# The output product of a mixer layer in three parts, the first as filling of the neighbourhood attention, and mixture-of-experts pairs opened before the previous pair is closed

## The chip, the cores and the metric

The kernel runs on one NeuronCore of a Trainium2 chip, in float32 inputs and outputs, as one launch. The metric is the device time of that launch in microseconds (us). Matrix products run on TensorE (PE in the profile, with its weight loads shown apart as PEld), elementwise work on VectorE (DVE), ScalarE (ACT) and GpSimd (POOL); SyncE (SP) issues nearly all of the DMAs. Each engine runs its own instructions in a fixed order and waits on semaphores.

## The reference, cut to what matters

The model is two blocks of two layers each, on 512 tokens of width 1024.

The first block's layers end in a mixture of experts where each expert chooses its tokens: 16 experts, 64 tokens each, inner width 512.

```
affinity = softmax(h @ w_router)
gate, idx = top_k(affinity.T, 64)                       # per expert
x_in = h[idx]                                           # 64 x 1024 per expert
y = (silu(x_in @ w_gate) * (x_in @ w_up)) @ w_down * gate
x = x + scatter_add(y, idx)
```

The second block's layers run four mixers on slices of 256 columns, side by side, and join them by one output product. There are 256 further tokens of context (`cx`), which are carried through layer 0 and serve only as keys and values in layer 1.

```
y_a = fourier_mix(...)                 # inputs 0..255 of the output product  (chunks 0, 1)
y_b = neighbourhood_attention(...)     # 256..511, 4 heads of 64             (chunks 2, 3)
y_c = spatial_gating(...)              # 512..767                            (chunks 4, 5)
y_d = diff_post(diff_latent(...))      # 768..1023, 4 heads of 64            (chunks 6, 7)
x  = x + g1 * (concat(y_a, y_b, y_c, y_d) @ w_out)
x  = x + g2 * (relu(h2 @ w_ff1)**2 @ w_ff2)
```

Before that, `ada_params` makes the modulation (g1 among them) from `silu(c) @ ada_w`, a product with a weight of 1024 x 6144 per layer.

## The kernel before, in words

**Number format.** Most weights and activations are split into a high and a low part (`wsplit`, `split`: a rounded copy on ACT, line 334 or 362, and the remainder on DVE, line 335 or 363), and a product is three matmuls (`mm3`: high by high, high by low, low by high, lines 353, 354, 356). The experts' weights are used unsplit, as plain float32; such a matmul shows as two PE instructions in the trace.

**Order of the work.** The kernel is written in a tile language. Python code traces instructions in an order; a scheduler then plays a timing model, gives each engine a fixed order (earlier traced work first among what its model holds ready) and puts each tile into one of the slots of its tag, as they come free. `k.fill(work, n)` steps a generator, so that pieces of other work are traced behind a given PE instruction. What the hardware does later can't change the order.

**Experts** (`experts`, from line 872; twice, once per layer). Four groups `g` of four experts. A group first gathers its tokens by a product with a one-hot matrix (line 888, 72 matmuls) and makes the gates and the transposed one-hot matrices (lines 899 to 915). Then it takes two pairs of experts. For each expert of a pair: gate and up product (line 930, both with 64 output columns, 32 PE instructions), a scaled copy to SBUF on ACT (`au`, 933), four transposes (936), silu on ACT (938) and a product on DVE (`gg`, 939). Then, for the pair, the down product (948): `G[h]` of the two experts write the two halves of the partitions of one PSUM tile, 32 PE instructions; its result is split (`yy`, 365 and 366), multiplied by the transposed one-hot matrix (956, 16 matmuls) and added to `x` (957). The weights come by DMA of 1 MiB (`we`, issued at line 288), 12 for a pair: 4 for each expert's gate and up and 4 for the pair's down weights. They have `NWE` = 14 slots in layer 0 and 12 in layer 1, at the right end of SBUF. Their rows in DRAM are 2 KB long.

**Second block** (`groups`, `na`, `diff`). After the projections, the neighbourhood attention `na` runs 24 units in layer 0 and 16 in layer 1 (a unit is one head and 128 queries): scores (1209, 1210; 256 columns each), bias add, softmax, four transposes (458), product with the values (492). Units alternate between the two heads of a pair `j`; the operands of the second pair are prepared at the first unit (`NAP`). Each pair's output goes through `parts` to chunks 2 and 3 of `YX` (and `YC` for the context).
Then `diff` runs as many units: two score tiles in PSUM (1292), two maxima (1295), two exponentials (1296), their combination (1302), six transposes and twelve value matmuls. Its first unit starts by `prepare`, which copies halves of queries and keys by DMA into stacked tiles (1252, tag `w`, 13 slots in all), and then `begin()`, which splits chunks 4, 5, 0, 1 with `parts`. From the third unit on it steps the output product: `adds` has 48 pieces, 8 output chunks `c` by 6 input chunks `e` (0 to 5), and `FILL[0]` = 2 are traced per unit. The rest follows behind `diff`, and then the last two input chunks (6, 7).
A piece is the three matmuls of `mm3` on 512 columns, and in layer 0 three more on the 256 context columns.

**PSUM** has 8 banks. `na` uses 4 for scores, 2 for transposes, 2 for outputs; `diff` 3 tiles of 2 banks (tag `pD`, which the pieces share) and 2.

Of the kernel before, what the change touches and what calls it, by code (L numbers as in the profile page):

```python
# [139 lines left out]
def layout(a):  # L140
# [18 lines left out]
    for n in ("ln_ffn", "sgu_ln_g_2", "sgu_ln_b_2", "sgu_b_2", "diff_lq1_2", "diff_lk1_2", "diff_lq2_2",  # L159
              "diff_lk2_2", "w_gate", "w_up", "w_down", "ada_w_2"):  # L160
        o[n] = a[n]
    for l in range(2):
# [23 lines left out]
        o[f"w2_out{l}"] = chunks(a["w_out_2"][l][:768], 2)  # L186
        o[f"w2_last{l}"] = chunks(a["w_out_2"][l][768:], 8)
# [12 lines left out]
NWE = (14, 12)  # L200
FIN = 0
NAP = 0
FILL = (2, 0, 0)
# [4 lines left out]
NAB = 7  # L208
# [10 lines left out]
HEADS = {"h": 18, **NORMS}  # L219
MIX = {"f": 4, "e": 3, "pt": 4, "sqm": 3, "lat": 6, "kg": 4, "qk": 12, "kr": 2, "vg": 2, "vm": 1, "wk": 2,  # L220
       "rope1": 1, "rope2": 1, "perm": 1, "wrt": 1}
# [15 lines left out]
P_WIN = {"pS": 4, "pT": 2, "pO": 2}  # L237
# [11 lines left out]
class Kernel:  # L249
# [622 lines left out]
    def experts(k, l, routed):  # L872
        nc = k.nc
        slots, slot, (aH, aL), T = routed
        for g in range(4):
            oh = []
            for t in range(4):
                o = k.t("oh", (128, 4, 64), F32R)
                nc.vector.tensor_tensor(o, slots, slot[:, t, 4 * g:4 * g + 4].unsqueeze(2).to_broadcast([128, 4, 64]),
                                        op=OP.is_equal)  # L880
                oh.append(o.rearrange("p e s -> p (e s)"))
            xin = [k.t("xin", (128, NK, 128)) for _ in range(2)]
            for c in range(NK + 1):
                p = k.ps("mm")
                for t in range(4):
                    for j in range(2):
                        w = T[t][j][:, c * 128:c * 128 + 128] if c < NK else (aH, aL)[j][:, t, :]
                        nc.tensor.matmul(p[:w.shape[1], :256], w, oh[t], start=(t == 0 and j == 0), stop=(t == 3 and j == 1))  # L888
                if c < NK:
                    gain = k.gain(("ln_ffn", l), c)  # L890
                    nc.vector.tensor_scalar(xin[0][:, c], p[:, :128], gain, None, op0=OP.mult)
                    nc.scalar.activation(xin[1][:, c], p[:, 128:256], AF.Copy, scale=gain)
                else:
                    ga = k.t("ga", (17, 256))
                    nc.vector.tensor_copy(ga, p[:17, :256])
            gates, roots, ohT = [], [], []
            for pr in range(2):
                p = k.ps("T")
                nc.tensor.transpose(p[:, :17], ga[:, pr * 128:pr * 128 + 128], k.ident[:17, :17])
                gt = k.t("s1", (128, 1))  # L900
                for h in range(2):
                    a = slice(64 * h, 64 * h + 64)
                    e = 4 * g + 2 * pr + h
                    nc.vector.tensor_copy(gt[a], p[a, e:e + 1])
                    r = k.t("s1", (128, 1))
                    for b in (slice(0, 64), slice(64, 128)):
                        nc.vector.tensor_copy(r[b], p[a, 16:17])
                    roots.append(r)
                gates.append(gt)
                p = k.ps("T")  # L910
                for t in range(4):
                    nc.tensor.transpose(p[:, t * 128:(t + 1) * 128],
                                        oh[t][:, pr * 128:pr * 128 + 128].bitcast(F32), k.ident)
                o = k.t("ohT", dt=F32R)
                nc.scalar.activation(o, p, AF.Copy)
                ohT.append(o)
            for pr in range(2):
                G = []
                for h in range(2):
                    e = 4 * g + 2 * pr + h  # L920
                    s = slice(h * 64, h * 64 + 64)
                    W = {}
                    for n in ("w_gate", "w_up"):
                        for kh in range(2):
                            W[n, kh] = k.load("we", k.i[n][l, e, kh * 512:kh * 512 + 512].rearrange(
                                "(c p) f -> p c f", p=128), (128, 4, 512))
                    p = k.ps("mm")
                    for c in range(NK):
                        for a, n in ((0, "w_gate"), (64, "w_up")):
                            nc.tensor.matmul(p[a:a + 64], xin[pr][:, c, s], W[n, c // 4][:, c % 4],  # L930
                                             start=(c == 0), stop=(c == NK - 1))
                    au = k.t("au")
                    nc.scalar.activation(au, p, AF.Copy, scale=roots[2 * pr + h])
                    p = k.ps("T", (128, 4, 128))
                    for t in range(4):
                        nc.tensor.transpose(p[:, t, :], au[:, t * 128:(t + 1) * 128], k.ident)
                    gg = k.t("gg", (128, 4, 64))
                    nc.scalar.activation(gg, p[:, :, 0:64], AF.Silu)
                    nc.vector.tensor_mul(gg, gg, p[:, :, 64:128])  # L939
                    G.append(gg)  # L940
                WD = [[k.load("we", k.i["w_down"][l, 4 * g + 2 * pr + h, :, half * 512:half * 512 + 512].rearrange(
                    "(c p) f -> p c f", p=128), (128, 4, 512)) for h in range(2)] for half in range(2)]
                yH, yL = k.t("yy", (128, D), F32R), k.t("yy", (128, D), F32R)
                for half in range(2):
                    p = k.ps("mm")
                    for t in range(4):
                        for h in range(2):
                            nc.tensor.matmul(p[64 * h:64 * h + 64], G[h][:, t, :], WD[half][h][:, t],  # L948
                                             start=(t == 0), stop=(t == 3))
                    s = slice(half * 512, half * 512 + 512)  # L950
                    k.split(p, yH[:, s], yL[:, s], scale=gates[pr])
                for cols in (HALVES if l and g == 3 and pr == 1 else (ALL,)):
                    for c in range(NK):
                        p = k.ps("mm")[:, cols]
                        for y in (yH, yL):
                            nc.tensor.matmul(p, y[:, c * 128:c * 128 + 128], ohT[pr][:, cols], start=(y is yH), stop=(y is yL))  # L956
# [230 lines left out]
    def na(k, l, P, parts, v, bias, ctx, emit):  # L1187
# [7 lines left out]
        def scores(u):  # L1195
# [3 lines left out]
            if u == units[NAB]:  # L1199
                for i in (2, 3):  # L1200
                    bias[i] = k.bias(l, i)
# [526 lines left out]
```

## Time and profile before

| | us |
|---|---|
| three timed runs | 3127.49, 3131.39, 3134.98; median 3131.39 |
| profiled execution | 3128.51, of which the span from the first to the last instruction is 3126.7 |
| PE busy | 2971.6 (95% of the span), PEld 2241.4 |
| DVE, ACT, POOL busy | 1581.2 (51%), 1205.4 (39%), 280.7 (9%) |
| DMA | 422.34 MB, mean 135 GB/s |
| mean granted TensorE clock | 0.970 of full speed |

Times inside the execution are us from the span's start. The stages that the change touches lie about there: experts of layer 0 from 463 to 742, of layer 1 from 1193 to 1478; neighbourhood attention of the second block's layer 0 from 1668 to 1725, `diff` and the rest of the output product to 1880; in layer 1 from 2587 to 2630 and on to 2740.

A busy PE is not a PE at its peak: a matmul's length in the trace includes its way through the array, and the next one starts before it ends. What counts is the distance from start to start.

### The profile page before, as it was taken

Reading aid. Unit: us, or ns where it says so; the run is one execution under the profiler, and the core shown is the slowest. Engines: PE = TensorE matmul, PEld = TensorE weight load, DVE = VectorE, ACT = ScalarE, POOL = GpSimd, SP = SyncE. Lnnn points to the kernel's source line nnn. Section 1 sums busy time; section 2 is a strip of 40 time slices with the busy share of each in tenths; the row PEclk is TensorE's granted clock in tenths of the full one; section 3 lists DMA queues with packets and bytes.
Section 4 is the critical chain, followed back from the end, with each engine's and each line's share of the span. In section 5 each row is a group of like instructions: output and inputs, shape, how many; then the busy total and the mean of one; then the engine's idle time right before and its main releaser. Section 6 shows DMA issues by size and latency. Waiting matters only on the chain.

```text
span 3126.7 us, 42254 instructions
## 1 busy us (share of the span) xinstructions
PE 2971.6 (95%) x16816; PEld 2241.4 (72%) x16816; DVE 1581.2 (51%) x3071; ACT 1205.4 (39%) x2356; POOL 280.7 (9%) x281
## 2 busy tenths in 40 slices
PE   8999979998999988999998899999999998999998
PEld 5677764444666864444887778888888787878887
DVE  5666652224576644234537666334344547654444
ACT  4646431113565532113426554222222336542332
POOL 2111120001102101001300011000000100010000
PEclk9999989999999998999999899999999998999999
DMA  5423249994433228996222311111111222222221
GB/s 183 135 95 122 95 180 332 358 370 172 161 109 115 82 78 316 367 370 242 62 74 70 90 41 55 68 55 68 68 54 54 97 96 71 65 81 95 94 98 64
DMA packets 168756, 422.34 MB, mean 135 GB/s; under 512 B 12144, under 2 KB 21616, under 8 KB 152816
## 3 DMA queue, kind: packets, MB, share of 16 engines
q1 hardware_dynamic: 167536, 416.76, 37.9%
q0 software_dynamic: 1024, 2.89, 0.4%
q8 instruction: 133, 2.18, 0.3%
q14 instruction: 63, 0.52, 0.0%
HBM read 405.18 MB, written 2.10 MB: 130 GB/s over the span
## 4 chain that ended last, share of the span: by engine, by line
PE 89%; DVE 4%; ACT 3%; issue 1%; DMA 1%; POOL 0%; SPq 0%; POOLq 0%; ACTq 0%; DVEq 0%
PE pmm L354 12%; PE pmm L353 12%; PE pmm L356 12%; PE pmm L930 8%; PE pS L353 5%; PE pS L356 4%; PE pS L354 4%; PE pmm L948 4%; PE pT L458 4%; PE pO L704 3%; PE pmm L888 2%; PE pA L998 2%; PE pmm L956 2%; PE pT L492 2%; PE pT L394 1%
## 5 line engine op out<-in xcount | busy, mean ns | idle before, releaser
L334 ACT ACTIVATE wh<-wr 128x1024 fp32r<-128x1024 f32 (+1 forms) x195 | 202.3, 1038 | 533.7 <-PE pmm L354 364.9
L335 DVE TENSOR_TENSOR wl<-wr,wh 128x1024 fp32r<-128x1024 f32 (+1 forms) x195 | 242.0, 1244 | 279.4 <-ACT wh L334 279.0
L930 PE MATMUL pmm<-we,xin 128*64 128x512 f32 x1024 | 238.1, 596 | 0.0
L353 PE MATMUL pS<-h,wh 128*128 128x512 f32 (+1 forms) x480 | 190.0, 400 | 12.5 <-ACT wh L334 10.2
L1616 DVE SCALAR_TENSOR_TENSOR x<-pmm,ada,x 128x512 f32<-128x512 f32 (+1 forms) x136 | 95.5, 717 | 206.4 <-PE pmm L356 206.3
L354 PE MATMUL pmm<-h,wh 128*128 128x512 f32 (+1 forms) x480 | 186.1, 389 | 2.7 <-DVE h L1036 2.6
L354 PE MATMUL pS<-h,wh 128*128 128x512 f32 (+1 forms) x480 | 185.2, 386 | 3.3 <-DVE h L366 3.3
L356 PE MATMUL pS<-h,wl 128*128 128x512 f32 (+1 forms) x480 | 185.2, 390 | 1.9 <-DVE wl L335 1.9
L356 PE MATMUL pmm<-h,wl 128*128 128x512 f32 (+1 forms) x480 | 184.0, 385 | 0.0
L353 PE MATMUL pmm<-h,wh 128*128 128x512 f32 (+1 forms) x480 | 182.9, 390 | 0.9 <-ACT h L1031 0.9
L334 ACT ACTIVATE vh<-wr 128x1024 fp32r<-128x1024 f32 x68 | 71.8, 1060 | 272.9 <-PE pmm L354 237.3
L930 PEld LDWEIGHTS pmm<-we,xin 128*64 128x64 f32 x1024 | 72.8, 137 | 136.8 <-issue 128.8
L379 POOL TENSOR_TENSOR sq<-sq,sq 128x512 f32<-128x512 f32 (+1 forms) x49 | 61.0, 1245 | 1174.7 <-ACT sq L371 1137.6
L948 PE MATMUL pmm<-we,gg 128*64 128x512 f32 x512 | 143.1, 605 | 15.1 <-DVE gg L939 15.1
L460 ACT ACTIVATE pt<-pT 128x512 f32<-128x512 f32 (+1 forms) x200 | 109.6, 554 | 118.9 <-PE pT L458 118.4
L335 DVE TENSOR_TENSOR vl<-wr,vh 128x1024 fp32r<-128x1024 f32 x68 | 83.7, 1233 | 114.0 <-ACT vh L334 114.0
L353 PE MATMUL pmm<-hid,vh 128*128 128x512 f32 (+1 forms) x400 | 139.3, 348 | 0.0
L439 DVE TENSOR_REDUCE s<-pS 128x1 f32<-128x512 f32 (+1 forms) x200 | 124.2, 622 | 27.8 <-PE pS L356 22.0
L354 PE MATMUL pmm<-hid,wh 128*128 128x512 f32 (+1 forms) x400 | 133.9, 350 | 0.0
L354 PE MATMUL pmm<-hid,vh 128*128 128x512 f32 (+1 forms) x400 | 133.8, 347 | 0.0
L353 PE MATMUL pmm<-hid,wh 128*128 128x512 f32 (+1 forms) x400 | 131.3, 349 | 0.0
L446 ACT ACTIVATE e<-pS,s,rt 128x512 f32<-128x512 f32 (+1 forms) x160 | 117.4, 734 | 17.6 <-DVE s L441 17.2
(443 smaller groups left out, 7179.0 us busy)
## 6 DMA issues: line engine op xcount, KB each, us to landing
we<-in_w_gate_dram SPq DMA_DIRECT2D x64, 1024.0 KB, 11.1
we<-in_w_up_dram SPq DMA_DIRECT2D x64, 1024.0 KB, 10.6
we<-in_w_down_dram SPq DMA_DIRECT2D x64, 1024.0 KB, 13.5
wr<-in_w_ff_dram SPq DMA_DIRECT2D x64, 1024.0 KB, 4.8
wra<-in_ada_w_dram SPq DMA_DIRECT2D x96, 512.0 KB, 4.2
wr<-in_w_in_dram SPq DMA_DIRECT2D x27, 1024.0 KB, 4.8
wr<-in_w_o_dram SPq DMA_DIRECT2D x8, 1024.0 KB, 4.8
wr<-in_w_mkv_dram SPq DMA_DIRECT2D x8, 1024.0 KB, 4.9
```

What stands on the lines that cost most here:

```text
L334: k.nc.scalar.activation(H[:, :m], raw[:, a:a + m], AF.Copy)
L335: k.nc.vector.tensor_sub(L[:, :m], raw[:, a:a + m], H[:, :m].bitcast(F32))
L353: mm(p, wH, xH, start=(first and j == 0), stop=False)
L354: mm(p, wH, xL, start=False, stop=False)
L356: mm(p, wL, xH, start=False, stop=(end and j == n - 1))
L439: nc.vector.reduce_max(m, s, axis=AX, negate=True)
L446: nc.scalar.activation(e, s, AF.Exp, bias=m, scale=1.0 if scale is None else scale, accum_out=z)
L458: k.nc.tensor.transpose(p[:, t - a, :], src[:, t * 128:(t + 1) * 128], k.ident)
L460: k.nc.scalar.activation(dst[:, a:b], p[:, :b - a, :], AF.Copy)
L930: nc.tensor.matmul(p[a:a + 64], xin[pr][:, c, s], W[n, c // 4][:, c % 4], start=(c == 0), stop=(c == NK - 1))
L948: nc.tensor.matmul(p[64 * h:64 * h + 64], G[h][:, t, :], WD[half][h][:, t], start=(t == 0), stop=(t == 3))
L1616: nc.vector.scalar_tensor_tensor(x, p, mod[:, 40 + o, j:j + 1], x, op0=OP.mult, op1=OP.add)
```

## The change

1. **Experts.** `experts` is cut into `gather` (a group), `opened` (a pair's gate and up products, to `gg`) and `closed` (its down product, to the add to `x`). The pair n+1 is opened before pair n is closed. Slots: `xin` 3 for 2, `gg` 4 for 3, `ohT` 3 for 2, `NWE` 13 and 11 for 14 and 12.
2. **Layouts.** `w_gate`, `w_up`, `w_down` and `ada_w_2` are laid out in DRAM so that each DMA reads one block, with 8 KB (4 KB for `ada_w_2`) in a row of a partition where it was 2 KB.
3. **Output product.** Three parts by input chunk: part 0 is chunks 0, 1, 4, 5 (32 pieces), traced inside `na`; part 1 is chunks 2, 3 (16 pieces), traced inside `diff`, one piece per unit; part 2 is chunks 6, 7, as before.
4. **`na` head by head.** Units go through head 0 (its 4 query blocks, and 2 of the context in layer 0), then head 1, and so on; heads 0 and 1 are prepared in the projections, 2 and 3 one head ahead. PSUM: 3 scores, 2 transposes, 1 output, 1 `pD`.
5. **Splits.** `parts` of chunks 4, 5, 0, 1 stand ahead of `na`; their remainders, those of `halves` and half of those of `keys` go to POOL.
6. **SBUF.** The first block's weight tiles (`WTS2`) move from the right end to the left; the mixer's own tiles (`MIXO`) lie last on the left; a tile `edge` of 96 bytes a partition stands at the right end.

```diff
-NWE = (14, 12)
+NWE = (13, 11)
-FILL = (2, 0, 0)
+FILL = (1, 0, 0)
-ROUTED = {"ht": 8, "ap": 2, "slots": 1, "oh": 4, "ga": 1, "xin": 2}
+ROUTED = {"ht": 8, "ap": 2, "slots": 1, "oh": 4, "ga": 1, "xin": 3}
-EXP = {"au": 2, "gg": 3, "yy": 3, "ohT": 2}
+EXP = {"au": 2, "gg": 4, "yy": 3, "ohT": 3}
-P_WIN = {"pS": 4, "pT": 2, "pO": 2}
+P_WIN = {"pS": 3, "pT": 2, "pO": 1, "pD": 1}
...
+    for n in ("w_gate", "w_up"):
+        o[n] = np.ascontiguousarray(a[n].reshape(2, 16, 2, 4, 128, 512).transpose(0, 1, 2, 4, 3, 5))
+    o["w_down"] = np.ascontiguousarray(a["w_down"].reshape(2, 16, 4, 128, 2, 512).transpose(0, 1, 4, 3, 2, 5))
...
+        o[f"w2_out0{l}"] = chunks(np.concatenate([w[:256], w[512:768]]), 4)
+        o[f"w2_out1{l}"] = chunks(w[256:512], 8)
+        o[f"w2_out2{l}"] = chunks(w[768:], 8)
...
+    def closed(k, l, n, G, gate, ohT):
+        nc = k.nc
+        WD = [[k.load("we", k.i["w_down"][l, 2 * n + h, half], (128, 4, 512)) for h in range(2)] for half in range(2)]
+        yH, yL = k.t("yy", (128, D), F32R), k.t("yy", (128, D), F32R)
+        for half in range(2):
+            p = k.ps("mm")
+            for t in range(4):
+                for h in range(2):
+                    nc.tensor.matmul(p[64 * h:64 * h + 64], G[h][:, t, :], WD[half][h][:, t], start=(t == 0), stop=(t == 3))
+            s = slice(half * 512, half * 512 + 512)
+            k.split(p, yH[:, s], yL[:, s], scale=gate)
...
     def experts(k, l, routed):
+        left = None
         for g in range(4):
+            for pr, (xin, gate, roots, ohT) in enumerate(k.gather(l, g, routed)):
+                G = k.opened(l, 2 * g + pr, xin, roots)
+                if left is not None:
+                    k.closed(l, *left)
+                left = 2 * g + pr, G, gate, ohT
+        k.closed(l, *left)
...
-        nc.vector.tensor_sub(low[other], src[rows], dst[rows].bitcast(F32))
+        nc.gpsimd.tensor_copy(low[other], low[rows].bitcast(F32))
...
-    def na(k, l, P, parts, v, bias, ctx, emit):
+    def na(k, l, P, heads, v, bias, ctx, emit, other, steps):
-        units = [(j, lo, qc, h) for j in range(2) for lo, nq in ranges for qc in range(nq) for h in range(2)]
+        units = [(g, lo, qc) for g in range(4) for lo, nq in ranges for qc in range(nq)]
...
+            if lo == 0 and qc == 0 and 0 < g < 3:
+                j, h = (g + 1) // 2, (g + 1) % 2
+                heads[g + 1] = k.na_prepare(P["nq", j], P["nk", j], h, ctx)
+                bias[g + 1] = k.bias(l, g + 1)
...
+            due = steps * max(0, n + 1 - 1) // (len(units) - 1)
+            k.fill(other, due - done[0])
+            done[0] = due
             return k.softmax(s, 256 * len(keys), tag="h")
...
-            if h == 0 and qc == 0:
+            if (j, lo) not in o:
                 o[j, lo] = k.ps("O")
...
     def halves(k, y, n):
         parts = [k.t("w", (128, S + C), F32R) for _ in range(2)]
-        k.split(y[:, :n], parts[0][:, :n], parts[1][:, :n])
+        k.nc.scalar.activation(parts[0][:, :n], y[:, :n], AF.Copy)
+        k.nc.gpsimd.tensor_sub(parts[1][:, :n], y[:, :n], parts[0][:, :n].bitcast(F32))
...
+            def adds(part):
+                for c in range(NK):
+                    yield from add(c, part, both)
...
             with vals, k.scope(f"pd{l}", P_WIN, PSUM):
-                k.na(l, P, na, V["nv"], bias, not last, lambda j, lo, n, o: parts(2 + j, lo, n, o))
+                for c in (4, 5, 0, 1):
+                    parts(c, 0, S, Y[c][:, :S], nc.gpsimd)
+                    if not last:
+                        parts(c, S, C, Y[c][:, S:], nc.gpsimd)
+                work = adds(0)
+                k.na(l, P, na, V["nv"], bias, not last, lambda j, lo, n, o: parts(2 + j, lo, n, o), work, 4 * NK)
+                for _ in work:
+                    pass
...
-                adds = both_adds()
-                k.diff(l, P, halves, dv, nlam, not last, begin, lambda j, lo, n, y: parts(6 + j, lo, n, y), adds)
+                work = adds(1)
+                k.diff(l, P, halves, dv, nlam, not last, lambda j, lo, n, y: parts(6 + j, lo, n, y), work)
```

## Rows read from the trace of the kernel before

**Rows 1.** Busy by engine in one group of four experts, layer 0.

```profile
535.10:603.50 68.40, 66.54 (x324) 31.23 (x324) 20.40 (x50) 10.95 (x22) 0.00 (x0) 1.00 1.00 365
```

**Rows 2.** Timeline of PE, one pair of experts: start, length, what, count, idle before.

```profile
574.30 13.10 PE L930 MATMUL pmm<-we,xin 128*64 128x512 f32 x60
...
588.91 1.93 PE L948 MATMUL pmm<-we,gg 128*64 128x512 f32 x4
590.77 0.66 PE L936 MATMUL pT<-c_ident,au 128*128 128x128 f32 x4
592.36 7.08 PE L948 MATMUL pmm<-we,gg 128*64 128x512 f32 x28 [0.93 <-DVE gg L939]
599.37 4.16 PE L956 MATMUL pmm<-ohT,yy 128*128 128x512 f32 x16
603.39 2.77 PE L888 MATMUL pmm<-oh,ht 128*128 128x256 f32 x21
```

**Rows 3.** Timeline of the weight loads in a down product.

```profile
564.12 0.14 PEld L948 LDWEIGHTS pmm<-we,gg 128*64 128x64 f32 x2 [0.28 <-issue]
...
568.84 0.14 PEld L948 LDWEIGHTS pmm<-we,gg 128*64 128x64 f32 x1 [0.29 <-issue]
```

**Rows 4.** Waits of PE over the span: total us, times, longest.

```profile
PE pmm L948 <- DVE gg L939: 15.1, 16, 1.0
PE pS L1209 <- ACT h L446: 11.7, 4, 6.9
PE pD L1292 <- DMA w<-w: 10.6, 2, 5.4
```

**Rows 5.** Windows of steady loading; last two columns: share of the DMA engines, GB/s.

```profile
500.00:530.00 30.00, 29.07 (x125) 11.05 (x123) 7.12 (x12) 3.52 (x6) 0.00 (x0) 1.00 1.05 386
99.80:102.20 2.40, 2.40 (x18) 1.15 (x17) 1.23 (x1) 2.36 (x4) 0.00 (x0) 1.00 0.78 328
```

**Rows 6.** Issue to landing of the experts' 1 MiB loads, 478 to 740.

```profile
DMA to landing us min/median/max: 5.4/12.2/16.4
```

**Rows 7.** The same of 1 MiB loads with 8 KB rows (w_ff).

```profile
DMA to landing us min/median/max: 4.6/4.8/5.1
```

**Rows 8.** Timeline of SP: the first loads into freed slots, layer 0.

```profile
478.23 0.92 SPq L288 DMA_DIRECT2D we<-in_w_up_dram  x2
```

**Rows 9.** Timeline of PE: the first product behind the experts of layer 0.

```profile
744.30 0.51 PE L353 MATMUL pS<-h,wh 128*128 128x512 f32 x1 [2.14 <-ACT wh L334]
```

**Rows 10.** Windows: PE, PEld, DVE, ACT, POOL busy, granted clock, DMA share, GB/s.

```profile
1668.00:1735.00 67.00, 49.60 (x343) 40.76 (x342) 47.82 (x121) 37.01 (x96) 4.16 (x8) 0.88 0.24 64
1735.00:1848.00 113.00, 109.88 (x721) 92.50 (x721) 79.29 (x158) 65.49 (x166) 7.01 (x10) 0.97 0.22 58
2587.00:2637.00 50.00, 39.35 (x270) 33.76 (x268) 34.40 (x83) 27.26 (x60) 2.48 (x5) 0.89 0.22 59
```

**Rows 11.** Timeline of PE: first matmul of two successive pieces, layer 0.

```profile
1855.13 0.40 PE L353 MATMUL pD<-h,wh 128*128 128x512 f32 x1
...
1856.18 0.40 PE L353 MATMUL pD<-h,wh 128*128 128x512 f32 x1
```

**Rows 12.** Waits of SP, 1640 to 1740.

```profile
SPq L1252 <- DVE hc L363: 42.2, 1, 42.2
```

**Rows 13.** Lines 1295, 1296, 1302 (min/median/max ns).

```profile
L1295 DVE TENSOR_REDUCE s<-pD x80: 404/948/958, 1727.3 to 2701.2; 128x1 f32<-128x768 f32 x64, 128x1 f32<-128x256 f32 x16
L1296 ACT ACTIVATE e<-pD,s x80: 464/896/912, 1728.3 to 2703.5; 128x768 f32<-128x768 f32 x64, 128x256 f32<-128x256 f32 x16
L1302 DVE SCALAR_TENSOR_TENSOR e<-e,s x40: 485/1018/1020, 1736.4 to 2705.2; 128x768 f32<-128x768 f32 x32, 128x256 f32<-128x256 f32 x8
```

**Rows 14.** Timeline of PE at the end of `diff`, layer 0.

```profile
1851.46 0.65 PE L492 MATMUL pT<-pt,dv 128*64 128x128 f32 x4 [0.53 <-ACT pt L460]
...
1861.17 1.21 PE L353 MATMUL pD<-h,wh 128*128 128x512 f32 x3 [1.39 <-ACT h L362]
```

**Rows 15.** Line 843: a POOL subtraction on 128x512.

```profile
L843 POOL TENSOR_TENSOR ht<-raw,ht x16: 1251/1260/1277, 448.0 to 1183.8; 128x512 fp32r<-128x512 f32 x16
```

More of the change, by code (lines that the diff above doesn't have):

```diff
@@ L870, in route, with gather @@
         return slots, slot, (aH, aL), T
-    def experts(k, l, routed):
+    def gather(k, l, g, routed):
         nc = k.nc
         slots, slot, (aH, aL), T = routed
-        for g in range(4):
[L876 to L956, printed above, removed]
-                        nc.vector.tensor_add(k.x[c][:, cols], k.x[c][:, cols], p)
@@ new lines, in gather @@
+        oh = []
+        for t in range(4):
+            o = k.t("oh", (128, 4, 64), F32R)
+            nc.vector.tensor_tensor(o, slots, slot[:, t, 4 * g:4 * g + 4].unsqueeze(2).to_broadcast([128, 4, 64]),
+                                    op=OP.is_equal)
+            oh.append(o.rearrange("p e s -> p (e s)"))
+        xin = [k.t("xin", (128, NK, 128)) for _ in range(2)]
+        for c in range(NK + 1):
+            p = k.ps("mm")
+            for t in range(4):
+                for j in range(2):
+                    w = T[t][j][:, c * 128:c * 128 + 128] if c < NK else (aH, aL)[j][:, t, :]
+                    nc.tensor.matmul(p[:w.shape[1], :256], w, oh[t], start=(t == 0 and j == 0), stop=(t == 3 and j == 1))
+            if c < NK:
+                gain = k.gain(("ln_ffn", l), c)
+                nc.vector.tensor_scalar(xin[0][:, c], p[:, :128], gain, None, op0=OP.mult)
+                nc.scalar.activation(xin[1][:, c], p[:, 128:256], AF.Copy, scale=gain)
+            else:
+                ga = k.t("ga", (17, 256))
+                nc.vector.tensor_copy(ga, p[:17, :256])
@@ L1254, in stacks, with diff @@
         return out
-    def diff(k, l, P, parts, v, nlam, ctx, begin, emit, other):
+    def diff(k, l, P, parts, v, nlam, ctx, emit, other):
         nc = k.nc
@@ L1278, in scores @@
                 prepare(0, 1)
-                begin()
             if j == 0 and units.index(u) == len(units) // 2 - NXT:
@@ L1449, in projections @@
         values_.enter_context(k.scope(f"nat{l}", NAT))
-        na = {0: k.na_prepare(P["nq", 0], P["nk", 0], not last, ("na", "nc"))}
+        na = {h: k.na_prepare(P["nq", 0], P["nk", 0], h, not last) for h in range(2)}
         bias = {h: k.bias(l, h) for h in range(2)}
@@ new lines, in adds @@
+            def adds(part):
+                for c in range(NK):
+                    yield from add(c, part, both)
+            both = ((0, ALL),) if last else ((0, ALL), (1, CTX))
+            with vals, k.scope(f"pd{l}", P_WIN, PSUM):
+                for c in (4, 5, 0, 1):
[6 more added lines that the diff above has]
+                    pass
@@ L1572, in both_adds @@
-                def both_adds():
-                    for c in range(NK):
-                        yield from add(c, True, both)
-                both = ((0, ALL),) if last else ((0, ALL), (1, CTX))
-                adds = both_adds()
-                k.diff(l, P, halves, dv, nlam, not last, begin, lambda j, lo, n, y: parts(6 + j, lo, n, y), adds)
+                dv = [V["dv"][128 * t] for t in range(4)] + [V["dv"]["c", t] for t in range(2)]
+                work = adds(1)
+                k.diff(l, P, halves, dv, nlam, not last, lambda j, lo, n, y: parts(6 + j, lo, n, y), work)
@@ L1578, in groups @@
                 mark(k, f"out{l}")
-                for _ in adds:
+                for _ in work:
                     pass
-                w[1] = k.weights(k.i[f"w2_last{l}"][0])
                 k.F = [k.pairs("h", S)] if last else [k.pairs("h", S), k.pairs("hc", C)]
```

173 lines of the change are left out of this document (106 added, 67 removed).

## The prediction

> **What bounds the kernel now.** I read the page's busy shares first: PE is busy for 95% of the span, so only what PE does, or what it waits for, can matter. The list of PE's waits comes next [rows 4]: it is short. Three entries lie in places that the change touches: 16 waits of the down product for `gg` (15.1 us), the first score matmuls of the neighbourhood attention waiting for exponentials (11.7), and `diff`'s first scores waiting for the DMAs of the stacked operands (10.6). A busy PE can still be a slow one, so I then read start-to-start distances in timelines, and windows by stage for the granted clock.
>
> In the experts' stage a group of four takes 68.40 us, PE is busy for 66.54 of it, and the DMA engines are at share 1.00 with 365 GB/s [rows 1]. Both are near their limit, so each has to be checked against the other. In the neighbourhood attention PE is idle for 17.4 us of 67 in layer 0 and 10.65 of 50 in layer 1, with a mean granted clock of 0.88 and 0.89, so part of each stretch ran at 1.2 instead of 2.4 GHz; in `diff` PE is busy for 109.9 of 113 [rows 10]. So `diff` is bound by PE and the neighbourhood attention partly is not, and the change carries work from the one to the other.
>
> **Experts in pairs.** A pair takes 603.39 - 574.30 = 29.09 us [rows 2]. In order: 14.61 to 588.91 (64 gate and up instructions and the first expert's transposes), 1.86 for 4 instructions of the down product, 1.59 for the second expert's transposes and 0.93 idle until its `gg`, 7.01 for the other 28, 4.02 for the scatter product. The 4 early instructions are the first expert's alone, since the second expert's `gg` isn't there yet. What that costs is seen in the weight loads [rows 3]: where both experts' instructions alternate, two weight loads start per 0.43 us (they write different halves of the partitions); where one expert's stand alone, one does. So 4 lone ones at the start and 4 at the end take eight steps of 0.43, and would take four if paired.
>
> After the change both `gg` of pair n are ready when its down product begins, because the opening of pair n+1 lies between. What remains is 14.61 + 0.58 (second transposes, by the 0.66 of the same rows less overlap) + 16 x 0.43 = 6.88 + 4.02 = 26.1. That is 3.0 us less, for 16 pairs 48 us. Nothing is added on PE; the last pair has no following one, but its two `gg` are old by then. From below the gain is the visible idle time alone, 15 [rows 4], if the scheduler still leaves the instructions unpaired. I take the upper end, since the code traces the two experts alternately and both are ready.
>
> Then the loads must keep up. A group would take 62.4 us for 24 MiB, 403 GB/s, while steady loading now shows 386 [rows 5], 2.72 us for 1 MiB. The stock of slots decides. In layer 0 the first slot comes free at 478.2 [rows 8]; with 13 loaded by then, 83 remain: the first lands 5.4 us later [rows 6], 82 more take 82 x 2.72 = 223 us, and behind the last one 7.5 us of work are left (half the down product, 3.44, and the scatter, 4.02): 714.1. PE alone would be done at 742.2 (744.30 less 2.14 [rows 9]) - 24 = 718.2. So the loads are just hidden. Layer 1 has two slots fewer, so its loads end 5.4 later against the same work: 1 to 2 us over. I take 46 us.
>
> The packed layout could make a load shorter: alone, a 1 MiB load lands in 5.4 us at best with 2 KB rows [rows 6] and 4.6 with 8 KB rows [rows 7]. As the loads are hidden at 2.72, that is worth 0 to 2 us; it could also be worse, as a 2.4 us window with 8 KB rows showed only 328 GB/s [rows 5]. `ada_w_2` has no wait of note; 0.
>
> A rule of the Trainium skill speaks against this part: "DMA: Bandwidth & Descriptors", section "Where 436 GB/s comes from", says that for transfers from HBM the HBM side binds at about 358 GB/s for a core. The trace doesn't agree, with 386 over 30 us [rows 5]. By the rule a load takes 2.93 us, the stage ends at 731.3 in layer 0 and 5.9 later than that in layer 1, and the 46 shrink to 16.
>
> **Moved weight tiles.** The 2.14 us wait for `wh` behind layer 0's experts [rows 9] comes where those tiles lay in the region of the experts' slots. On the left their place is free after the last gather. I take 2 us (0 to 4, with the next wait).
>
> **Output product: what moves.** A piece takes 1.05 us in layer 0 [rows 11]; in layer 1, without the context's 256 of its 768 columns, about two thirds, 0.70 (estimate). 32 pieces go into `na`: 33.6 and 22.4 us.
>
> *Into `na`.* Of the idle time, the wait for the DMA stacks (5.4 in layer 0, 5.2 in layer 1) is its last part, which leaves 12.0 and 5.4 to fill. One or two pieces per unit can take most of it, not all: the start still waits for exponentials before there is a value product. I take 9 and 4, and 2 each for a clock that falls less. One PSUM tile for pieces means that a chunk's first piece waits for the add of the chunk before; 8 times a layer, I take 1 us (0 to 8). `na` grows by 24 - 0.4 = 23.6 and 17.4.
>
> The splits on POOL take 1.26 us a piece [rows 15], some 20 us a layer with `halves` and `keys`, beside PE. The first piece needs the third of them; the tiles are ready since the projections. Uncovered it would cost up to 8 us at the start of layer 0. Preparing by head adds no instruction; heads 2 and 3 come six units ahead of use. 0.
>
> *Into `diff`.* SP waited 42.2 us, until `parts` of `begin()` let go of tiles of the tag `w` [rows 12]; only then could the stacks be loaded. After the change `parts` comes before `na`, so the stacks load during it. The waits of 10.6 [rows 4] go, with some half-speed time behind them: 7 and 6 us.
>
> *Inside `diff`.* 22 units lose a piece or more each: 44 pieces before, 16 after, so 28 x 1.05 = 29 us of PE in layer 0. What is late next is the softmax of a unit: one maximum, two exponentials and the combination in a row are 0.95 + 0.90 + 0.90 + 1.02 = 3.8 us [rows 13], with the small operations and handovers about 4.3 (estimate). Now the 113 us are 4.7 for the average of 16 full and 8 shorter context units, with two pieces in each; less 1.2 us of pieces that is 3.5, under the chain of a full unit. So the chain binds by a little: I take 22 back of 29. In layer 1, 14 units lose 14 x 0.70 = 9.8, of which I take 5.
>
> *Behind `diff`.* 4 pieces (4.2 us) in layer 0 and 20 (14 us) in layer 1 were left over there; after it, none and 2: 4.2 and 12.6 less. But they were the cover of the last normalisation: from the last value product (1852.1) to the last inputs' use (1861.17) 9.1 us pass, with only 1.39 of idle time before it [rows 14]. Uncovered, about 4 us come back in layer 0 and 6 in layer 1 (the clock may fall too); 9 each at worst.
>
> Sum, layer 0: 23.6 - 7 - 22 - 4.2 + 4 = -5.6. Layer 1: 17.4 - 6 - 5 - 12.6 + 6 = -0.2. Together -6; at best -28 (all idle time of the two windows [rows 10]), at worst +44 (no idle time filled, the units' pace unchanged, 9 us of tail each: 33.6 - 7 - 4.2 + 9 and 22.4 - 6 - 12.6 + 9).
>
> **Sum.** -46 - 2 - 6 = -54 on the profiled execution's 3128.5: 3074.5. That execution lies 2.9 under the median of the timed runs, 3131.4; on the median 3077.
>
> **Rivals.**
> (a) *The down products stay unpaired*, and only the visible waits go: -15 - 2 - 6 = -23, 3108. For it: the order is the scheduler's, which already put four lone instructions early because its model held them ready. Against: with pair n+1's opening ahead, both experts are ready.
> (b) *The softmax chain sets `diff`'s pace already*: pieces put into `na` cost their full time and come back only in part, +30: 3131.4 - 46 - 2 + 30 = 3113. For it: DVE is busy for 79 us of `diff`'s 113 in layer 0. Against: PE is busy for 110.
> (c) *The loads become the bound, and the kernel slower.* At 328 GB/s, the lowest stretch with 8 KB rows [rows 5], a load takes 3.20 us: layer 0's experts end at 478.2 + 5.4 + 82 x 3.20 + 7.5 = 753.5, 11.3 later than now, layer 1's 17.7 later. With the -8 of the rest +21: 3152. It decides from 3.07 us a load (166 loads against a gain of 502 us at no load time, and the 8). For it: the stage is at share 1.00 now and gets fewer slots. Against: the quick landing of 8 KB rows [rows 7], and 386 GB/s with short ones.
> (d) *A cap between*, 2.93 us a load: -16 - 2 - 6 = -24, 3107. Its mechanism is (c)'s at a milder price; the 386 [rows 5] is against it. This is the skill's HBM limit named above.
>
> **How the numbers follow.** Forecast 0.64 (its own range 3057 to 3099: experts 40 to 50, output product -20 to +8, moved tiles 0 to 4), (a) 0.12, (b) 0.08, (c) 0.06, (d) 0.04, and 0.06 for more gain than that range. The range 3052 to 3110 takes in (a) and (d) and leaves out (c), most of (b) and the far side. Faster or slower means by over 0.2% (6 us), what a measurement of this kernel can tell from no change: slower 0.07 ((c), and a little of (b) with a short gain), same 0.04, faster 0.89.
>
> **What would show it.** Experts: a pair in 26 us, the waits for `gg` gone, lone loads of the down product rare; a group in 62 to 63 us at about 400 GB/s. If PE shows waits for `we` instead, (c) or (d). `na` longer by 17 to 24 us with a granted clock above 0.95, no wait for the stacks, `diff` in some 90 us with PE below 97% busy. The prediction is wrong if the pair stays above 28 us, or if `diff` keeps its 113.

## The result and the profile after

The changed kernel takes 3092.65 us (median of four runs, 3089.93 to 3095.38) where the kernel before took 3131.01 beside it: ratio 0.9877, interval 0.986 to 0.9894, so 38.4 us less. Forecast were 3077 us, 54 less, with a range of 3052 to 3110. The profiled execution took 3094.44 us, its span is 3092.7 (before 3126.7).

Where the 34.0 us of the span went, from the starts of the first and last matmuls of each stretch in both timelines (us):

| stretch | before | after | change | forecast |
|---|---|---|---|---|
| start to the first gather, layer 0 | 463.2 | 461.4 | -1.8 | 0 |
| experts, layer 0 (gather to last scatter) | 279.0 | 268.2 | -10.8 | -23 |
| to the first gather, layer 1 | 450.9 | 447.9 | -3.0 | -2 |
| experts, layer 1 | 284.8 | 277.8 | -7.0 | -23 |
| to the first score of `na`, layer 0 | 191.1 | 189.0 | -2.1 | 0 |
| `na`, to the first score of `diff` | 56.5 | 84.6 | +28.1 | +23.6 |
| `diff`, first to last score | 114.8 | 86.8 | -28.0 | -29 |
| to the first product on the hidden layer | 83.1 | 80.5 | -2.6 | -0.2 |
| to the first score of `na`, layer 1 | 663.6 | 659.3 | -4.3 | 0 |
| `na`, layer 1 | 41.4 | 58.7 | +17.3 | +17.4 |
| `diff`, layer 1 | 72.1 | 62.4 | -9.7 | -11 |
| to the first product on the hidden layer | 78.4 | 72.5 | -5.9 | -6.6 |
| the rest | 347.8 | 343.6 | -4.2 | 0 |

The forecast's 7 and 6 us for the waits for the stacks stand in the rows of `diff`, since before the change that wait comes behind its first scores:

```profile
1725.46 0.63 PE L1292 MATMUL pD<-w,w 128*128 128x256 f32 x3
1731.48 2.26 PE L1292 MATMUL pD<-w,w 128*128 128x256 f32 x9 [5.39 <-DMA w<-w]
```

The sign is as forecast, the experts gave 17.8 us of 46, and 15.4 us came from stretches for which 0 or -2 was forecast. So that the time comes as near to the forecast as it does is in part luck: the experts fell short by 28 us, and gains that were not forecast stood in for half of it.

The waits of PE over the span after the change (total us, times, longest):

```profile
PE pT L402 <- DVE sq L387: 11.0, 5, 5.3
PE pmm L964 <- ACT yy L373: 9.3, 12, 0.8
PE pD L361 <- ACT h L1529: 6.9, 2, 5.7
```

The waits for `gg` and for the stacks [rows 4] are gone. In their place the scatter product waits twelve times for the split of the down product (before: twice, 1.6 us), and the first pieces behind `diff` wait for its last output.

The windows that answer to [rows 10] and [rows 1] (start:end, length, PE, PEld, DVE, ACT, POOL busy, granted clock, DMA share, GB/s), cut at the stretches of the table, then two groups of experts:

```profile
1644.30:1728.90 84.60, 77.08 (x514) 65.99 (x513) 57.81 (x126) 41.29 (x96) 18.85 (x23) 0.98 0.31 88
1728.90:1815.70 86.80, 78.61 (x536) 64.54 (x534) 72.61 (x149) 59.29 (x153) 6.15 (x9) 0.96 0.18 46
2614.20:2676.60 62.40, 55.73 (x379) 45.25 (x379) 52.68 (x89) 43.67 (x102) 5.12 (x8) 0.97 0.17 39
2676.60:2749.10 72.50, 55.67 (x368) 50.57 (x367) 43.98 (x80) 36.77 (x75) 16.00 (x17) 0.86 0.16 59
...
580.70:648.20 67.50, 65.12 (x324) 30.62 (x324) 20.99 (x50) 10.96 (x22) 0.00 (x0) 1.00 0.95 393
516.20:580.70 64.50, 64.50 (x323) 30.46 (x322) 20.35 (x50) 10.96 (x22) 0.00 (x0) 1.00 0.98 404
```

The same cut of layer 0 before the change:

```profile
1669.00:1725.50 56.50, 45.28 (x323) 37.10 (x321) 41.39 (x111) 31.90 (x82) 1.70 (x3) 0.91 0.18 50
1725.50:1840.30 114.80, 105.69 (x691) 89.59 (x690) 79.77 (x156) 64.94 (x163) 9.48 (x15) 0.94 0.27 71
1840.30:1923.40 83.10, 76.86 (x445) 63.92 (x444) 56.19 (x95) 44.97 (x87) 20.84 (x18) 0.94 0.15 51
```

`na` now runs at a granted clock of 0.98 (0.91 before) with 7.5 us of idle PE time, and `diff` is less bound by PE: 8.2 of its 86.8 us are idle in layer 0, 6.7 of 62.4 in layer 1. Of the experts' groups in layer 0 the second takes 64.5 us, the third 67.5, hardly less than the 68.40 before [rows 1]; the two middle ones of layer 1 take 67.4 and 69.2. The forecast's sign was 62 to 63.

A timeline of PE in a later pair shows why (start, length, line, operation, count, idle before):

```profile
702.00 0.59 PE L957 MATMUL pmm<-we,gg 128*64 128x512 f32 x1
702.42 0.59 PE L935 MATMUL pmm<-we,xin 128*64 128x512 f32 x1
702.43 4.02 PE L957 MATMUL pmm<-we,gg 128*64 128x512 f32 x15
706.38 0.66 PE L941 MATMUL pT<-c_ident,au 128*128 128x128 f32 x4
706.96 1.07 PE L957 MATMUL pmm<-we,gg 128*64 128x512 f32 x2
707.97 2.11 PE L964 MATMUL pmm<-ohT,yy 128*128 128x512 f32 x8
710.01 3.65 PE L957 MATMUL pmm<-we,gg 128*64 128x512 f32 x14
714.43 1.89 PE L964 MATMUL pmm<-ohT,yy 128*128 128x512 f32 x7 [0.78 <-ACT yy L373]
```

The 32 instructions of one down product are no longer cut by a wait, but by other work: a gate product, the transposes of the next pair, half of the scatter product of this one. One of the cuts mostly falls behind an odd number of the experts' alternating matmuls, so that these, which run side by side when they are neighbours [rows 3], stand alone on both sides of it: 14 of the 16 down products have 4 to 8 instructions without their partner (the expectation below says 15). Some of these run beside a gate matmul; quite alone stand 26 and 28 instructions a layer, against 52 and 46 before. Counted over all pairs by start-to-start distance, idle time behind them included, the down products take 70.2 and 73.9 us a layer, against 72.7 and 72.6 before. Fully paired, eight would take 8 x 6.88 = 55.

### The profile page after: what moved, and what is told of

Its sections match the earlier page's. It is cut to its first block, busy times and chain, and to the rows that moved or that the text cites. A ratio compares the mean times of both kernels' runs of the same rounds, so it can differ in the third digit from the quotient of the medians.

```text
span 3092.7 us, 42292 instructions
## 1 busy us (share of the span) xinstructions
PE 2941.6 (95%) x16816; PEld 2228.6 (72%) x16816; DVE 1579.8 (51%) x3055; ACT 1202.0 (39%) x2352; POOL 324.8 (11%) x318
## 4 chain that ended last, share of the span: by engine, by line
PE 88%; DVE 5%; ACT 3%; DMA 1%; issue 1%; POOL 1%; SPq 0%; POOLq 0%; DVEq 0%; ACTq 0%
PE pmm L362 12%; PE pmm L361 12%; PE pmm L364 12%; PE pmm L935 8%; PE pS L361 5%; PE pS L362 4%; PE pS L364 4%; PE pmm L957 4%; PE pT L466 3%; PE pO L712 3%; PE pmm L896 2%; PE pmm L964 2%; PE pA L1016 2%; PE pT L500 1%; PE pT L402 1%; PE pD L361 1%
## 5 line engine op out<-in xcount | busy, mean ns | idle before, releaser
L343 DVE TENSOR_TENSOR vl<-wr,vh 128x1024 fp32r<-128x1024 f32 x68 | 83.1, 1224 | 116.6 <-ACT vh L342 116.6
L447 DVE TENSOR_REDUCE s<-pS 128x1 f32<-128x512 f32 (+1 forms) x200 | 124.4, 623 | 27.6 <-PE pS L364 21.7
L957 PE MATMUL pmm<-we,gg 128*64 128x512 f32 x512 | 134.0, 597 | 0.0
L454 ACT ACTIVATE e<-pS,s,rt 128x512 f32<-128x512 f32 (+1 forms) x160 | 117.5, 735 | 18.5 <-DVE s L449 18.1
```

The lines of the kernel that those rows point to most:

```text
L343: k.nc.vector.tensor_sub(L[:, :m], raw[:, a:a + m], H[:, :m].bitcast(F32))
L447: nc.vector.reduce_max(m, s, axis=AX, negate=True)
L454: nc.scalar.activation(e, s, AF.Exp, bias=m, scale=1.0 if scale is None else scale, accum_out=z)
```

## Experiments

**Is it the order?** Edges of order alone (no semaphore) tie the PE instructions of the experts into one sequence (the diff is cut; the comments stand for its other lines):

```diff
+    def behind(k, later, earlier):
+        k.tc.add_manual_dep(later.ins, earlier.ins.name, mybir.DependencyInfo(
+            mybir.DependencyClass.NoSync, mybir.DependencyReason.DATA), reason="order on TensorE")
 # closed: each down matmul behind the one before, the first behind the opening of the next pair,
 # the next pair's last four transposes behind the last of them, the scatter product behind these
```

> The changed kernel with one thing more: edges of order alone (no semaphore) on TensorE, so that a pair runs as 24 gate and up matmuls, the four transposes, 8 gate and up, the 16 matmuls of the down product of the pair before with nothing between them, the four transposes, 16 of the scatter product. Theory A (the part of the forecast gain that did not come was lost to the order in which the scheduler puts the instructions: transposes or a scatter that cut a pair of experts' matmuls apart, 4 to 8 lone matmuls in 15 of 16 down products, and waits for the split of a first half): a pair takes 26 to 26.5 us instead of about 28.9 on average, each layer's experts take 13 to 20 us less, the time is 3055 to 3068. Theory B (the loads set the pace by now, and the order only follows them): waits of the gate and up products for `we` take the place of what the order saves, 15 us or more over both layers, and the time is 3083 to 3095.

Measured: 3059.54 us (3055.86 to 3068.38), ratio to the kernel before 0.9779 [0.976, 0.9798], within theory A. The experts take 258.5 and 261.3 us, 9.7 and 16.5 less than in the changed kernel; of the other 6.8 us of the span, 5.6 lie ahead of the first gather, where the edit does nothing and kernels differ by as much. A pair in PE's timeline:

```profile
547.27 10.52 PE L940 MATMUL pmm<-we,xin 128*64 128x512 f32 x48
557.72 0.66 PE L952 MATMUL pT<-c_ident,au 128*128 128x128 f32 x4
558.30 3.65 PE L940 MATMUL pmm<-we,xin 128*64 128x512 f32 x16
561.79 7.04 PE L968 MATMUL pmm<-we,gg 128*64 128x512 f32 x32
568.75 0.66 PE L952 MATMUL pT<-c_ident,au 128*128 128x128 f32 x4
569.17 4.11 PE L981 MATMUL pmm<-ohT,yy 128*128 128x512 f32 x16
573.14 1.09 PE L896 MATMUL pmm<-oh,ht 128*128 128x256 f32 x7
```

And two windows of steady loading, the columns as above:

```profile
520.00:700.00 180.00, 180.00 (x898) 82.63 (x896) 54.94 (x132) 29.38 (x58) 0.31 (x1) 1.00 0.95 391
1240.00:1400.00 160.00, 160.00 (x804) 73.84 (x802) 52.20 (x122) 29.61 (x60) 0.00 (x0) 1.00 0.99 408
```

A pair takes 573.14 - 547.27 = 25.87 us, the down product 568.75 - 561.79 = 6.96. PE is busy for all of both windows, and its list of waits has none for `we`. So the order is shown to be the cause, and the loads are not. Of the 26.2 us, the lone instructions account for some 11.6 (estimate: 54 of them, two to a step of 0.43) and PE's waits in the experts' products for some 8 (14.2 before the edit, 6.1 behind it); the rest, the further cuts, was not measured by itself.

**The pairs by themselves.** The same kernel as the changed one, but each pair closed behind its own opening:

```diff
                 G = k.opened(l, 2 * g + pr, xin, roots)
-                if left is not None:
-                    k.closed(l, *left)
-                left = 2 * g + pr, G, gate, ohT
-        k.closed(l, *left)
+                k.closed(l, 2 * g + pr, G, gate, ohT)
```

> The changed kernel with the down and scatter product of a pair right behind its own opening, as before the change; packed weights, slots, and the rest of the change stay. Theory A (the later closing is what shortened the experts' stages by 10.8 and 7.0 us, by the visible waits for `gg`): those waits come back, 14 to 15 us, the stages take 279 and 285 us again, the time is 3108 to 3112. Theory B (the packed weights shortened the stages, by quicker loads): the stages keep most of their gain and the time is 3091 to 3098.

Measured: 3111.13 us (3108.77 to 3114.21), theory A. The stages take 278.8 and 285.6 us, and the wait is back:

```profile
PE pmm L957 <- DVE gg L944: 13.9, 15, 0.9
```

The later closing is worth 18.5 us in the changed kernel, the visible wait and little more; with the forced order, 51.6, of which 44.6 lie in the experts' stages.

**The rows of the weight loads.** With the forced order, `w_gate`, `w_up` and `w_down` laid out as before:

```diff
-            W = {(name, kh): k.load("we", k.i[name][l, 2 * n + h, kh], (128, 4, 512))
+            W = {(name, kh): k.load("we", k.i[name][l, 2 * n + h, kh * 512:kh * 512 + 512].rearrange(
+                "(c p) f -> p c f", p=128), (128, 4, 512))
...
```

> The changed kernel with the forced order, and w_gate, w_up and w_down in their old layout (rows of 2 KB instead of 8 KB in the weight loads); `ada_w_2` stays packed. Theory A (a load hides as long as it takes under some 2.7 us, in either layout): 3057 to 3063, no waits for `we`. Theory F (rows of 2 KB reach no more than the 386 GB/s of the kernel before, while the forced order now asks for 406): 96 MiB a layer take 261 us instead of 248, the stage grows by up to 10 us a layer, waits for `we` show: 3066 to 3082.

Measured: 3069.04 us (3062.39 to 3076.02), ratio 0.9805 [0.9788, 0.9822], in theory F's range, but not where it said. Layer 0's experts take 258.5 us as with 8 KB rows, layer 1's 265.0, 3.7 more. The other 3.3 us of the span are spread over stretches that the edit doesn't touch (2.7 of them ahead of the first gather, a stretch that takes 455.7 to 461.4 us in kernels that all do the same there). The two windows again:

```profile
520.00:700.00 180.00, 180.00 (x903) 83.29 (x902) 53.27 (x131) 30.09 (x60) 0.31 (x1) 1.00 1.05 386
1240.00:1400.00 160.00, 159.04 (x792) 74.56 (x790) 49.53 (x115) 27.31 (x56) 0.00 (x0) 1.00 1.05 387
```

The wait for loads in layer 1:

```profile
PE pmm L969 <- DMA we<-in_w_down_dram: 1.9, 2, 1.0
```

With 2 KB rows the DMA engines are at share 1.05 with 386 GB/s, with 8 KB rows they reach 408 at 0.99. Layer 0, with thirteen slots, shows no wait for a load; layer 1, with eleven, does.

**The filling of `na`.** No piece in `na`, two per unit in `diff` again (the diff is cut):

```diff
-FILL = (1, 0, 0)
+FILL = (2, 0, 0)
-                k.na(..., work, 4 * NK)
+                k.na(..., None, 0)
-                work = adds(1)
+                work = chain(adds(0), adds(1))
```

> The changed kernel with no piece of the output product in the neighbourhood attention: the 32 pieces of the first part go into the differential attention again, two pieces a unit, ahead of the second part. The early splits of `parts` and the early loads of the stacks stay. Theory C (the filling costs more than it brings: between the experts' output and the feed-forward both layers together changed by only -0.8 us, though the waits for the stacks of 10.6 us went): those waits stay away, `diff` takes about 105 us again in layer 0, and the time is 3079 to 3088. Theory D (the filling uses time in which TensorE was idle, and is what pays for the tails): 3096 to 3106.

Measured: 3092.84 us (3091.61 to 3103.34), the same as with 32 pieces, between both theories. `diff` takes 108.5 us in layer 0 (its window stands below); `na` and `diff` of layer 1:

```profile
2556.50:2602.30 45.80, 37.16 (x258) 31.08 (x256) 34.09 (x78) 27.69 (x61) 7.10 (x10) 0.93 0.31 84
2602.30:2669.30 67.00, 63.55 (x418) 52.63 (x418) 56.00 (x91) 45.65 (x104) 5.12 (x8) 0.97 0.20 52
```

**Fewer pieces in `na`.** The last two output chunks of part 0, 8 pieces, go to `diff` and behind it (the diff is cut):

```diff
-                work = adds(0)
+                work = adds(0, 0, 6)        # chunks 0 to 5; na: 24 steps
...
-                work = adds(1)
+                work = chain(adds(0, 6), adds(1))
```

> The changed kernel with the last 8 of the 32 pieces of the first part held back from the neighbourhood attention: they run in the differential attention and behind it, ahead of the second part (layer 0: 22 in units, 2 behind; layer 1: 14 in units, 10 behind). Theory C (in `diff` the chain of the softmax sets the pace, with 8.2 and 6.7 us of idle TensorE time, and the uncovered tail has another 5 to 9 us at half clock, while in the neighbourhood attention a piece costs its full time): the neighbourhood attention gets 8 and 5 us shorter, `diff` and its tail take the pieces for little: 3080 to 3087. Theory D (a piece costs the same wherever it stands): 3090 to 3095.

Measured: 3083.52 us (3081.7 to 3083.79), theory C. `na`, `diff` and the rest up to the hidden layer, by windows of layer 0, first with no piece in `na` (`fill_undone`, the run above), then with 24 (32 stand above):

```profile
1642.00:1705.10 63.10, 47.65 (x322) 38.61 (x320) 44.48 (x106) 36.65 (x92) 19.03 (x23) 0.92 0.34 86
1705.10:1813.60 108.50, 103.61 (x691) 86.76 (x690) 82.83 (x160) 63.62 (x158) 6.14 (x9) 0.98 0.17 46
1813.60:1898.60 85.00, 76.90 (x445) 64.51 (x444) 57.53 (x98) 43.00 (x83) 21.33 (x18) 0.94 0.14 50
```

```profile
1644.10:1719.10 75.00, 68.45 (x467) 58.59 (x465) 53.23 (x121) 40.34 (x95) 19.14 (x23) 0.98 0.32 87
1719.10:1809.80 90.70, 82.95 (x564) 68.55 (x564) 73.45 (x148) 60.16 (x155) 6.14 (x9) 0.96 0.17 43
1809.80:1890.90 81.10, 73.27 (x426) 61.64 (x427) 55.34 (x97) 43.20 (x84) 20.76 (x18) 0.94 0.15 53
```

The first 24 pieces lengthen `na` by 11.9 us, 0.5 each, and shorten what follows by 21.7. The last 8 lengthen it by 9.6, 1.2 each, and shorten what follows by 4.5. Filling pays up to a point, and the change goes past it: with 0, 24 and 32 pieces the three windows sum to 256.6, 246.8 and 251.9 us (layer 1: 190.1, 187.5, 193.6).

**Both together, and more held.** The forced order with 8 pieces held, and with 16 (chunks 0 to 3 in `na`, the same edit with 4 for 6):

> The forced order of the experts and the 8 held pieces (two chunks) together, on the changed kernel. If the two are independent, as their stages are, the gains add: 3092.7 - 33.1 - 9.1 = 3050.4, between 3046 and 3055. If the one takes the other's gain (the clock, the queue of the loads): 3056 or more.

> As order_and_two_chunks, with 16 of the 32 pieces held back (four chunks). With none held the time is 3092.7, with 8 it is 3083.5, with all 32 it is 3092.8 (without the forced order). Theory C (the neighbourhood attention has room for some 16 to 24 pieces at less than their full time; what it can't hide should stand in `diff` up to its softmax pace): a flat optimum, 3046 to 3054. Theory E (only `diff`'s idle 15 us could take pieces, and 8 of them fill it): each further piece costs its full time there, 8 x 1.05 and 8 x 0.70 less what the neighbourhood attention saves at 0.5 a piece: 3055 to 3062.

Measured: 3048.01 us (3047.53 to 3052.09), ratio 0.9739 [0.9726, 0.9753], and 3051.17 (3044.28 to 3053.93). The gains add, and the optimum is flat between 16 and 24 pieces.

**The slots of PSUM.** `fill_undone` no longer waits for the stacks, yet its three windows are no shorter than before the change. It was run again with the old slots (`P_WIN` of 4, 2 and 2), and the best kernel with a fourth score slot in layer 1, where a piece needs one bank:

> As fill_undone (no piece in the neighbourhood attention), and its PSUM slots as before the change: four for scores and two for the value products instead of three, one and the tile for pieces. It asks where the 10.6 us went that PE waited for the stacks before: they are gone in fill_undone too, yet its `na` to feed-forward takes 256.6 and 190.1 us against 254.4 and 191.9 before the change. Theory G (they were paid for with the slots that the pieces' tile took): the neighbourhood attention falls from 63.1 and 45.8 us to about 58 and 42, the time to 3082 to 3087. Rival H (the slots cost nothing; the order head by head and the early splits cost it): 3090 to 3095.

> As order_and_two_chunks, with a fourth slot for scores in layer 1, where a piece of 512 columns needs one bank, not two. Theory G (slots hold up the neighbourhood attention): layer 1's takes 2 to 4 us less, 3044 to 3046. Rival H: no change, 3047 to 3050.

Measured: 3086.52 us (3081.64 to 3089.24), 6.3 less and in theory G's range, but only part of it as G said: `na` takes 60.9 and 43.9 us, 2.2 and 1.9 less, half of what theory G asked. And 3054.72 (3052.45 to 3058.4): `na` of layer 1 takes 54.9 instead of 53.3, so no gain there. The 6.7 us more than the best kernel lie between the two layers' experts (452.1 against 444.2), which the edit does not touch; that stretch takes 446 to 449 us in most kernels here, and why it differs is not known.

**Two terms of forecast 0 and 2.** The differences of `parts` ahead of `na` on DVE, in the best kernel; and `WTS2` on the right again, with the forced order and without (`k.scope(f"wa{l}", WTS2, side="right")`):

> As order_and_two_chunks, with the differences of `parts` for the first part's inputs on VectorE instead of POOL. The forecast gave POOL's 1.26 us a piece no cost, or up to 8 us at the start of layer 0; the trace shows waits of 3.5 us there for POOL. Theory A (that wait is the whole cost): 1 to 4 us faster, 3044 to 3047. Rival (VectorE's 20 added pieces delay the first softmax as much): 3047 to 3052.

> The changed kernel with the forced order, and the weight tiles of the first block (`wr`, `wh`, `wl`) on the right side again, in the region of the experts' slots. Theory A (their move took away the wait of 2 us behind layer 0's experts, and some time at half clock with it): 2 to 4 us slower than with the forced order alone, 3061 to 3064. Rival (the early gather that now stands ahead, or the loads' earlier end, would have hidden it anyway): 3058 to 3060.

> The changed kernel (its own order of the experts) with the weight tiles of the first block on the right again. With the forced order their side made no difference. Forecast's term: 2 us slower for the wait behind layer 0's experts, with some half-speed time up to 4: 3094 to 3097. Rival (nothing, here too): 3090 to 3093.5.

Measured: 3046.81 us (3044.53 to 3050.71), 3060.92 (3059.29 to 3063.39) and 3093.88 (3089.91 to 3097.9). None can be told from the kernel that it was derived from. But the wait for `wh` behind layer 0's experts [rows 9] is gone with the tiles on the left and back with them on the right, here in `tiles_right` (4.89 us with the forced order):

```profile
732.40 0.80 PE L361 MATMUL pS<-h,wh 128*128 128x512 f32 x1 [5.20 <-ACT wh L342]
```

## Why the prediction was right, and where not

**Experts, the failed step.** "I take the upper end, since the code traces the two experts alternately and both are ready." Both were ready, as forecast, but so was other work, and the scheduler put it between them. The forecast's sum for a pair, 26.1, is right for the order that it assumed (25.87), and 20.5 and 23.5 us less a layer than before are the forecast 46 but for 2. In the changed kernel's own order 17.8 came, near the 15 of rival (a), and for its reason. By the forecast's own sign, a pair above 28 us, this part was wrong: with the 10.2 us of a group that are no pair (68.40 - 2 x 29.09), the four groups above give 28.5 a pair on average (estimate).

**Loads.** Hidden, as forecast: no load sets PE's pace at 393 to 408 GB/s. Rivals (c) and (d) are out. The rule that spoke against this part, from the Trainium skill, "DMA: Bandwidth & Descriptors", section "Where 436 GB/s comes from" (HBM binds at about 358 GB/s), would have given 3107; these windows, with 386 to 408 GB/s, don't agree with it.

**The packed layout** (0 to 2 us): it can't show in the changed kernel, where PE asks for less than either layout gives. With the forced order it is worth some 4 us in layer 1's experts.

**Moved tiles** (-2): the wait went, as forecast, but the time did not follow. The stretch got 3.0 us shorter, but with the tiles back it stays so within 1.1; from the first gather of layer 0 to that of layer 1, 716.1 us pass with the tiles on either side. With them on the left, the product starts right behind the last scatter matmul and waits for splits on VectorE instead (1.32 and 1.56 us). These are single traces, and that stretch differs by 3 us between most kernels here.

**`na` and `diff`** (-6): measured are -2.5 in layer 0 and +1.7 in layer 1. `fill_undone`, the change without the filling, takes this apart:

| term | layer 0 | forecast | layer 1 | forecast |
|---|---|---|---|---|
| waits for the stacks (`diff`, before to `fill_undone`) | -6.3 | -7 | -5.1 | -6 |
| `na` without any piece (the same two) | +6.6 | 0 | +4.4 | 0 |
| 32 pieces into `na` (`fill_undone` to the change) | +21.5 | +23.6 | +12.9 | +17.4 |
| 28 and 14 pieces out of `diff` | -21.7 | -22 | -4.6 | -5 |
| tail | -2.6 | -0.2 | -5.9 | -6.6 |

The step that failed is the 0 behind "Preparing by head adds no instruction", with the slots, for which the forecast had no term: `na` got longer before a piece was in it, by what the stack waits gave. The slots given up for the pieces' tile cost some 2 us a layer of it; the rest (the order head by head, or the early splits) was not separated. "I take 9 and 4" for idle time that the pieces fill, and 2 each for the clock, was a little low: 12.1 of 33.6 and 9.5 of 22.4 us did not show. In layer 0 the first 24 pieces filled it (11.9 us instead of 25), and the last 8 found none.

**The pace of `diff`**: "the chain binds by a little: I take 22 back of 29" held, with 21.7. With one piece a unit PE idles there, and 86.8 us are 3.6 a unit. Rival (b), by which the chain sets the pace already before the change, is out: with 28 pieces less `diff` got 21.7 us shorter, and the output product came to -0.8, not +30.

**The tail**: forecast 4 and 6 us uncovered. The two waits behind the last value products are 2.88 and 1.19 us in layer 0, 2.86 and 5.69 in layer 1, so 4.1 and 8.6. The granted clock falls behind the first of them, to 0.50 from 1829.6 to 1836.0 in layer 0 and 0.56 from 2694.5 to 2701.0 in layer 1:

```profile
1829.62 1.98 PE L427 MATMUL pT<-c_ident,rt 128*64 128x128 f32 x16 [2.88 <-DVE rt L416]
...
2701.68 1.01 PE L361 MATMUL pD<-h,wh 128*128 128x256 f32 x3 [5.69 <-ACT h L1529]
```

**What was not in the forecast**: 10.6 us in the projections and the feed-forward (-2.1, -4.3, -4.2), present in every kernel of this study that carries the change (some 9 to 12). In the feed-forward of layer 1 PE never waits and has its full clock, yet it starts more matmuls in the same time. Windows of 260 us, about 11 us behind the first product on the hidden layer, before and after:

```profile
2790.00:3050.00 260.00, 260.00 (x1132) 212.26 (x1131) 121.33 (x143) 76.80 (x96) 0.00 (x0) 1.00 0.27 97
```

```profile
2760.00:3020.00 260.00, 260.00 (x1143) 214.31 (x1142) 121.28 (x143) 76.72 (x96) 0.00 (x0) 1.00 0.28 97
```

By start-to-start distance, products with `wh` take 233.1 ns before and 230.5 after, with `wl` 233.4 and 225.8; those with `vh` and `vl`, the other pair of weight tiles, 226.8 and 227.2 before, 226.6 and 226.7 after. Summed over the three stretches without PE's idle time, products with `wh` and `wl` take 10.8 us less than before, those with `vh` and `vl` 0.2 less: the whole gain lies with these two tiles. `wh` and `wl` lie at the right end of SBUF there, `vh` and `vl` don't, and all that the change does to the former is `edge`, which moves them by 96 bytes. The address is thus the likely cause; a kernel with `edge` alone was not run, so it is argued and not shown.

## What to carry to other kernels

Being ready together does not make two instructions neighbours: where a gain rests on adjacency, read the issued order, and force it if it must hold. Work moved as filling pays while the receiving stage idles and no longer, so move it in portions and look for the point where a piece costs its full time. The best kernel here is the change with the forced order and 24 pieces in `na`, 3048 us, 83 less than before.

## What the runs showed of the hardware

- The same product of 128x512 took 225.8 to 227.2 ns a step with some weight tiles and 230.5 to 233.4 with others, all at full clock (1.00) and without a wait. The tiles differ in their place in SBUF; that this is the cause is not shown.
- With rows of 8 KB instead of 2 KB the same 1 MiB loads went from 387 to 408 GB/s in layer 1's window, and the DMA engines' share from 1.05 to 0.99.
- Going from the paired 64-column matmuls to full-width transposes cost about 0.1 us (6.96 us for 16 steps of 0.429). The Trainium skill, "TensorEngine Tiling (Array Packing)", section "Key Properties", says that a change of tiling mode drains the engine. The 0.1 us fit that; what they are spent on no run shows.
